# One pool moved ahead of another and the compressions moved to later projections, in a hybrid NSA and HGRN2 decoder layer

## The chip, the cores and the metric

The kernel runs on one core of one Trainium2 chip. The metric is the device time of one execution in microseconds (us), taken on that core. The kernel before was run three times for it: a median of 1119.54 us, from 1118.82 to 1120.39. One further execution was recorded by the hardware profiler; all rows below come from it.

The engines are named as in the profile: PE (TensorE: matmuls; PEld is its loading of weights), DVE (VectorE), ACT (ScalarE), POOL (GpSimd) and SP (SyncE, which here only issues DMAs). SPq, ACTq and POOLq are the DMA issues of these engines.

## What is computed

One decoder layer on x of 512 tokens by 2048. Cut to what matters here:

```python
h = rmsnorm(x, norm_in)
proj = h @ w_in                      # 2048 x 7728: q, six K/V pieces, gates, z, and HGRN2's q, f, i, z
kc = compress_blocks(k_cmp, pe_k, w1_k, w2_k)   # 31 blocks of 32 tokens, (blk + pe) -> gelu(@ w1) @ w2
vc = compress_blocks(v_cmp, pe_v, w1_v, w2_v)
o_a = attention over compressed, selected and windowed tokens   # 16 heads of 64, 4 K/V groups
o_h = hgrn2_mixer(q_h, f_h, i_h, lb)                            # 8 heads of 128, chunks of 64
mixed = concat(head_rmsnorm(o_a) * silu(z_a), head_rmsnorm(o_h) * silu(z_h))
out = rmsnorm(x + mixed @ w_out, final_norm)
```

Everything is float32, and the result has to agree with float32 arithmetic.

## The kernel before

**Products in three parts.** A float32 matmul of the projections is done as three faster ones: each operand is split into a high part and a low remainder (hi and lo), and the product is hi·hi + hi·lo + lo·hi. The transposed, normalised input is held as `hh0` to `hh3` (high) and `hl0` to `hl3` (low): eight tiles of 8192 bytes per partition (the function `b8`, pool "big"). A piece of the projection's weights is loaded by SP into a tile `w` of 4096 bytes (`load_raw`, L163; pool "w", `b4`), split by ACT (high part, L304) and DVE (low part, L305) into two more tiles `w`, and used by PE. There are ten tiles in that pool, so a load waits for a tile to come free.

**Three forms of projection.** In `proj_fm` (L545) `w` is the stationary operand and 512 columns (2048 bytes) of an `hh` or `hl` tile stream past it: L559, L560 and L561, `pj<-hh,w` in the rows, where the moving operand stands first and the weights second. One projection of 128 columns is 16 such triples in two halves of weights, 48 matmuls. In `proj_tm` (L566; L584 to L586) it is the other way: 128 columns of `hh` or `hl` are the weights, and `w` streams. `seven` (L456 to L458, L466 to L468) computes two of the projections from seven products instead of eight; it too streams `w`, past weights that are pieces of `hh` and `hl` or sums of such pieces in tiles `s`. Late in the kernel `hh2`, `hl2`, `hh3` and `hl3` hold the mixed result instead, for the output projection.

**Where the tiles lie.** Pools of tiles are laid out in the order of their creation: "const", then "big" (64 KiB per partition), then "small" (2,624 bytes of little tiles, `sm`), then the pools that come later, "w" among them. `hh0` therefore begins 65,536 + 2,624 = 68,160 bytes ahead of the first tile `w`. That is 133 × 512 + 64: since tiles `w`, `hh` and `hl` and the columns in them step by multiples of 512 bytes here, a piece of `w` that is used as weights lies 64 bytes past a multiple of 512 from the `hh` or `hl` columns that stream at that time, and the other way round in `proj_tm` (448 past one). The tiles `s` lie multiples of 512 from the tiles `w`.

**Order of the work.** `run` (L114) weaves generators: each yields an estimated cost after a piece of work, and the one that is furthest behind in cost divided by its weight goes next. The order in which instructions are written is the order of each engine's queue. From 271.5 us on the stage between the first projections and the attention runs (L1163 to L1177):

- `blocks` (L605) gathers the raw K (or V) to be compressed from DRAM into four tiles by eight DMAs (L611 to L614), for K on ACT's queue, for V on POOL's, clears a few columns (L619, POOL) and adds the position term, 16 operations on DVE (L625).
- `compress` (L629) loads the first weight matrix in four pieces (L632, SP) and the second (L637, SP), does 64 matmul records of 128x128 (L641), a gelu on ACT and DVE (L647 to L652), and the second product: L657 for K, which gives `kc_hi` and `kc_lo` (L659, L660), L670 for V (from two copies by ACT, L664).
- `make_q` and `make_kd` each do one projection by `proj_fm` and then `split_dma` (L683): one operation of DVE, one of ACT, one of DVE (L686 to L688) and DMAs on SP (L691). `make_kd(0, 1)` moreover copies `kc_hi` and `kc_lo` with POOL into the tiles `kw` (L711, L712), which the first scores read (L779).
- `rows_back` (L1076) reads values back from DRAM; here for `v_tok`, four DMAs on POOL's queue.

In the kernel before, the K compression is woven into kd00 and q0 (`make_kd(0, 0)` and `make_q(0)`, 22 : 10), the V compression into kd01, q1, kd10 and q2 (44 : 44). Then the attention of 16 heads is woven with the other projections as its filling (160 : 102): q3, kd11, q4 to q7 and `hgrn_qf(0)`, ten projections of 48 matmuls.

Of the kernel before, what the change touches and what calls it, by code (L numbers as in the profile page):

```python
# [48 lines left out]
def hymba_layer(ctx: ExitStack, tc: tile.TileContext, x, norm_in, w_in, pe_k, w1_k, w2_k,  # L49
                pe_v, w1_v, w2_v, lower_bounds, nsa_norm, hgrn_norm, w_out, final_norm, out):  # L50
    nc = tc.nc
# [3 lines left out]
    w_out2 = w_out.rearrange("l d c -> (l d) c")  # L55

    const = ctx.enter_context(tc.tile_pool(name="const", bufs=1))
    big = ctx.enter_context(tc.tile_pool(name="big", bufs=1))
    small = ctx.enter_context(tc.tile_pool(name="small", bufs=2))
    psum = ctx.enter_context(tc.tile_pool(name="psum", bufs=1, space=bass.MemoryType.PSUM))  # L60

    cnt = [0, 0, 0]
# [1 line left out]
    def nm(s):  # L64
        cnt[0] += 1
        return f"{s}_{cnt[0]}"
# [8 lines left out]
    def sl(dt=FP32):  # L75
        return space["slab"].tile([P, 512], dt, name=nm("s"), tag="s", bufs=NSLAB)
# [35 lines left out]
    def run(*gens):  # L112

        st = [[g, t, 0.0] for g, t in gens]  # L114
        while st:
            e = min(st, key=lambda e: e[2] / e[1])
            try:
                c = next(e[0])
                e[2] = max([o[2] / o[1] for o in st if o is not e]) * e[1] + 1e-6 if c is None else e[2] + c
            except StopIteration:  # L120
                st.remove(e)

    def chain(*gens):
        for g in gens:
            yield from g
# [479 lines left out]
    def blocks(acc, pcol, eng):  # L605

        kv = []
        for j in range(2):
            f = acc[j]
            e, o = sl(), sl()  # L610
            eng.dma_start(out=e[0:64, :], in_=f[0:64, :])  # L611
            eng.dma_start(out=e[64:128, 0:511], in_=f[0:64, 1:512])
            eng.dma_start(out=o[0:64, :], in_=f[64:128, :])
            eng.dma_start(out=o[64:128, 0:511], in_=f[64:128, 1:512])  # L614
            kv += [e, o]
        blk = [sl() for _ in range(4)]
        for uq in range(4):
            b4_ = blk[uq].rearrange("p (u g n) -> p u g n", u=4, g=4)
            nc.gpsimd.memset(b4_[:, :, :, 31:32], 0.0)  # L619
            pe = col[:, pcol + uq * 4:pcol + uq * 4 + 4].unsqueeze(2).broadcast_to([P, 4, 31])  # L620
            for g in range(4):
                src = kv[g].rearrange("p (n u two) -> p u n two", u=8, two=2)
                n0 = uq // 2
                sv = src[:, (uq % 2) * 4:(uq % 2) * 4 + 4, n0:n0 + 31, 0]
                nc.vector.tensor_tensor(b4_[:, :, g, 0:31], sv, pe, ALU.add)  # L625
        return blk
# [70 lines left out]
    def make_kd(g2, b):  # L697


        acc = []  # L700
        yield from proj_fm(acc, (C_KS, C_KW)[b] + g2 * P, P)
        if b == 0:
            t = [sl(F32R) for _ in range(4)]
            v = t
        else:
            t = [space["att"].tile([P, 672], F32R, name=nm("kw"), tag="kw", bufs=KWB) for _ in range(4)]
            v = [a[:, 160:672] for a in t]
            for i in range(4):
                g = 2 * g2 + i // 2
                src = (kc_hi, kc_lo)[i % 2]  # L710
                nc.gpsimd.tensor_copy(t[i][:, 0:P], kd[g][0][i % 2][:, 0:P].bitcast(FP32))  # L711
                nc.gpsimd.tensor_copy(t[i][:, P:160], src[:, g * 32:(g + 1) * 32].bitcast(FP32))  # L712
        split_dma(acc[0], 1.0, [(v[0], 0, 0, 0), (v[0], 1, 0, 0), (v[1], 0, 1, 0), (v[1], 1, 1, 0),
                                (v[2], 0, 0, 1), (v[2], 1, 0, 1), (v[3], 0, 1, 1), (v[3], 1, 1, 1)])
        kd[2 * g2][b], kd[2 * g2 + 1][b] = t[0:2], t[2:4]

    def make_q(p):
        acc = []
        yield from proj_fm(acc, C_Q + p * P, P)
        qe, qo = sl(F32R), sl(F32R)  # L720
        split_dma(acc[0], -DH ** -0.5, [(qe, 0, 0, 0), (qe, 1, 1, 0), (qo, 0, 0, 1), (qo, 1, 1, 1)])
        q2[2 * p], q2[2 * p + 1] = qe, qo
# [127 lines left out]
    def attention():  # L850
        units = [(h, i, b) for h in range(HEADS) for i in range(NT) for b in ((0, 1) if i else (None,))]
        es, ys_, behind = {}, {}, []

        def step(gen):
            return next(gen, None)

        for u in range(len(units) + AHEAD):
            if u < len(units):
                h, i, b = units[u]
                while q2[h] is None or kd[h // 4][1] is None:  # L860
                    yield None
                if h not in es:
                    es[h] = head_setup(h)
                ys_[u] = scores(es[h], i, b)
                yield (0.4, 0.24, 0.33, 0.44)[i]
            v = u - AHEAD
            if v >= 0:
                h, i, b = units[v]
                flip(es[h], i, b, ys_.pop(v))
                yield 0.11 * max(i + 1, 2)  # L870
                if behind:
                    c = next(behind[0], None)
                    if c is None:
                        behind.pop(0)
                    else:
                        yield c
                if b == 1 and i == 3:
                    weigh(es[h])
                    yield 2.5
                    behind.append(head_out(es.pop(h)))  # L880
                    if h % 4 == 3:
                        behind.append(attn_cmp(h // 4))
        for g in behind:
            yield from g
# [188 lines left out]
    def rows_back(scr_, alloc, eng=nc.sync):  # L1073
        tiles = [alloc() for _ in range(NT)]
        for t in range(NT):
            eng.dma_start(out=tiles[t], in_=scr_[t])  # L1076
        return tiles
# [74 lines left out]
    KC, VC, vf = [], [], []  # L1152
# [15 lines left out]
    kblk = blocks(kf, 32, nc.scalar)  # L1168
    masks()
    vc_bd += [sl() for _ in range(2)]  # L1170
    for v in vc_bd:
        nc.gpsimd.memset(v, 0.0)
    run((chain(make_kd(0, 0), make_q(0)), 22), (compress(kblk, w1_k, w2_k, True), 10))
    v_tok += rows_back(vt_scr, sl, nc.gpsimd)
    vblk = blocks(vf, 48, nc.gpsimd)
    run((chain(make_kd(0, 1), make_q(1), make_kd(1, 0), make_q(2)), 44), (compress(vblk, w1_v, w2_v, False), 44))
    fill = [make_q(3), make_kd(1, 1)] + [make_q(p) for p in range(4, 8)]  # L1177
    with tc.tile_pool(name="pt", bufs=2) as space["pt"]:
        run((attention(), 160), (chain(*fill, hgrn_qf(0)), 102))
    att.close()  # L1180
    space["late"] = ctx.enter_context(tc.tile_pool(name="late", bufs=NLATE))
    hv[0] = rows_back(v_scr[0], late)
# [1 line left out]
    fill = chain(hgrn_qf(1), hgrn_qf(2), hgrn_qf(3), z_proj(C_ZH, sz[2]))  # L1184
# [77 lines left out]
    for c in range(3):  # L1262
# [3 lines left out]
        p = proj_tm([], w_out2, mT, c * 512, 512, out_done(c))  # L1266
# [35 lines left out]
```

## Time and profile before

| | us |
|---|---|
| median of three runs (range) | 1119.54 (1118.82 to 1120.39) |
| the profiled execution | 1119.59 |
| span of its trace, first to last instruction | 1117.9 |
| PE busy in the span | 1087.6 (97%) |
| DVE busy | 659.5 (59%) |
| ACT busy | 419.9 (38%) |
| POOL busy | 95.3 (9%) |
| mean granted clock of TensorE | 0.993 of 2.4 GHz |

The span is divided below into stages by time: input and first projections to 97 us, `seven` to 271.5, the stage with the two compressions to 369, attention with its filling to 615, the HGRN2 heads with theirs to 925, then gates, z and output projections. A matmul's length in the rows is the time that it is in the array, some 0.39 us for 512 columns; since matmuls follow each other in a pipeline, the distance from one start to the next is what one costs.

### The profile page before, as it was taken

Reading aid. Unit: us, or ns where it says so; the run is one execution under the profiler, and the core shown is the slowest. Engines: PE = TensorE matmul, PEld = TensorE weight load, DVE = VectorE, ACT = ScalarE, POOL = GpSimd, SP = SyncE. Lnnn points to the kernel's source line nnn. Section 1 sums busy time; section 2 is a strip of 40 time slices with the busy share of each in tenths; the row PEclk is TensorE's granted clock in tenths of the full one; section 3 lists DMA queues with packets and bytes.
Section 4 is the critical chain, followed back from the end, with each engine's and each line's share of the span. In section 5 each row is a group of like instructions: output and inputs, shape, how many; then the busy total and the mean of one; then the engine's idle time right before and its main releaser. Section 6 shows DMA issues by size and latency. Waiting matters only on the chain.

```text
span 1117.9 us, 15221 instructions
## 1 busy us (share of the span) xinstructions
PE 1087.6 (97%) x5610; PEld 885.0 (79%) x5610; DVE 659.5 (59%) x1549; ACT 419.9 (38%) x835; POOL 95.3 (9%) x170
## 2 busy tenths in 40 slices
PE   7999999999889999999999999999999999999996
PEld 6799888888768777777677788888888788888886
DVE  4766757663434567675656466666667789424333
ACT  6534443341113555564544222222232443323212
POOL 1000000102310102020200000000000000102010
PEclk9999999999989999999999999999999999999998
DMA  9435346545565422222112223222121723235223
GB/s 316 143 113 170 104 144 214 166 141 171 159 180 152 132 57 57 57 76 57 39 39 71 80 76 97 76 74 76 57 76 57 245 76 119 97 116 176 96 85 123
DMA packets 100010, 127.45 MB, mean 114 GB/s; under 512 B 6672, under 2 KB 62368, under 8 KB 99936
## 3 DMA queue, kind: packets, MB, share of 16 engines
q1 hardware_dynamic: 94368, 113.90, 33.2%
q0 software_dynamic: 2624, 8.39, 2.2%
q10 hardware_dynamic: 2944, 4.19, 1.1%
q8 instruction: 44, 0.72, 0.3%
q14 instruction: 30, 0.25, 0.1%
HBM read 106.01 MB, written 12.06 MB: 106 GB/s over the span
## 4 chain that ended last, share of the span: by engine, by line
PE 88%; DVE 4%; issue 3%; DMA 2%; POOL 1%; ACT 1%; SPq 1%; ACTq 0%; POOLq 0%
PE pj L559 8%; PE pj L560 8%; PE pj L561 8%; PE pj L585 7%; PE pj L584 7%; PE pj L586 7%; PE ot L826 4%; PE pj L807 3%; PE lp L975 3%; PE pj L457 2%; PE pj L456 2%; PE pj L458 2%; DMA w<-in_w_in_dram 2%; PE lp L793 2%; PE lp L794 2%
## 5 line engine op out<-in xcount | busy, mean ns | idle before, releaser
L305 DVE TENSOR_TENSOR w<-w,w 128x1024 fp32r<-128x1024 f32 (+3 forms) x169 | 204.5, 1215 | 169.5 <-ACT w L304 76.0
L304 ACT CAST w<-w 128x1024 fp32r<-128x1024 f32 (+3 forms) x169 | 172.9, 1036 | 273.1 <-DMA w<-in_w_in_dram 137.8
L559 PE MATMUL pj<-hh,w 128*128 128x512 f32 x448 | 184.6, 412 | 4.9 <-ACT w L304 4.9
L560 PE MATMUL pj<-hl,w 128*128 128x512 f32 x448 | 180.6, 403 | 0.0
L561 PE MATMUL pj<-hh,w 128*128 128x512 f32 x448 | 179.6, 401 | 0.0
L584 PE MATMUL pj<-w,hh 128*128 128x512 f32 (+2 forms) x352 | 127.2, 361 | 0.0
L585 PE MATMUL pj<-w,hl 128*128 128x512 f32 (+2 forms) x352 | 126.2, 358 | 0.0
L586 PE MATMUL pj<-w,hh 128*128 128x512 f32 (+2 forms) x352 | 125.4, 356 | 0.0
L559 PEld LDWEIGHTS pj<-hh,w 128*128 128x128 f32 x448 | 84.8, 189 | 25.1 <-ACT w L304 5.4
L561 PEld LDWEIGHTS pj<-hh,w 128*128 128x128 f32 x448 | 84.7, 189 | 20.4 <-issue 1.3
L560 PEld LDWEIGHTS pj<-hl,w 128*128 128x128 f32 x448 | 84.8, 189 | 17.3 <-issue 1.0
L762 DVE CUSTOM_DVE_ANT_0 s<-s,lp 128x128 f32<-128x128 f32 (+3 forms) x128 | 60.3, 482 | 40.9 <-PE lp L794 30.1
L767 ACT ACTIVATE s<-s,mn 128x128 f32<-128x128 f32 (+3 forms) x128 | 71.6, 560 | 33.6 <-DVE mn L762 25.8
L586 PEld LDWEIGHTS pj<-w,hh 128*128 128x128 f32 x352 | 66.2, 188 | 8.9
L584 PEld LDWEIGHTS pj<-w,hh 128*128 128x128 f32 x352 | 66.2, 188 | 8.7
L585 PEld LDWEIGHTS pj<-w,hl 128*128 128x128 f32 x352 | 66.2, 188 | 8.0
L807 PE MATMUL pj<-ident,s 128*128 128x128 f32 x320 | 54.6, 276 | 1.0 <-ACT s L767 1.0
L826 PE MATMUL ot<-pt,s 128*64 128x512 f32 (+3 forms) x256 | 49.9, 441 | 0.8 <-DVE pt L818 0.8
L807 PEld LDWEIGHTS pj<-ident,s 128*128 128x128 f32 x320 | 39.6, 140 | 11.6 <-ACT s L767 5.3
L826 PEld LDWEIGHTS ot<-pt,s 128*64 128x64 f32 x256 | 24.4, 136 | 21.3 <-issue 9.4
L816 ACT COPY pt<-pj 128x256 f32<-128x256 f32 (+2 forms) x56 | 25.6, 457 | 41.3 <-PE pj L807 40.7
L584 PE MATMUL pj<-w,s 128*128 128x512 f32 x96 | 37.7, 393 | 0.0
(346 smaller groups left out, 1914.8 us busy)
## 6 DMA issues: line engine op xcount, KB each, us to landing
w<-in_w_in_dram SPq DMA_DIRECT2D x121, 512.0 KB, 3.5
w<-in_w_out_dram SPq DMA_DIRECT2D x32, 512.0 KB, 3.6
s<-s SPq DMA_DIRECT2D x48, 128.0 KB, 2.3
w<-in_x_dram SPq DMA_DIRECT2D x16, 256.0 KB, 6.5
d<-e POOLq DMA_DIRECT2D x12, 256.0 KB, 2.9
l<-in_x_dram SPq DMA_DIRECT2D x12, 256.0 KB, 5.1
out_dram<-l SPq DMA_DIRECT2D x12, 256.0 KB, 3.1
w<-in_w_in_dram SPq DMA_DIRECT2D x5, 456.0 KB, 3.3
```

The source lines that it names most:

```text
L304: nc.scalar.copy(hi, raw)
L305: nc.vector.tensor_tensor(lo, raw, hi.bitcast(FP32), ALU.subtract)
L559: nc.tensor.matmul(acc[j], wh, hh, start=kk == 0, stop=False)
L560: nc.tensor.matmul(acc[j], wh, hl, start=False, stop=False)
L561: nc.tensor.matmul(acc[j], wl, hh, start=False, stop=kk == NK - 1)
L584: nc.tensor.matmul(o, ah, hi[:, k, :], start=kk == 0, stop=False)
L585: nc.tensor.matmul(o, al, hi[:, k, :], start=False, stop=False)
L586: nc.tensor.matmul(o, ah, lo[:, k, :], start=False, stop=kk == NK - 1)
L762: nc.vector.tensor_tensor_reduce(out=y, in0=e["bias"][:, 384 - i * P:512], in1=lp, scale=1.0, scalar=3e38, op0=ALU.add, op1=ALU.min, accum ...
L767: nc.scalar.activation(y, y, AF.Exp, bias=mn, scale=-1.0, accum_out=e["ls"][:, 2 * i + b:2 * i + b + 1])
L807: nc.tensor.transpose(tps[:, j * P:(j + 1) * P], y[:, j * P:(j + 1) * P], ident)
L826: nc.tensor.matmul(e["ot"][b * 64:(b + 1) * 64, j * P:512], v_tok[j][:, b * 256 + g * DH:b * 256 + (g + 1) * DH], e["pt"][:, b, j * 512:38 ...
```

## The change

The pool "small" is created ahead of "big". `hh0` moves back by 2,624 bytes, the tiles `w` stay where they are, and `hh0` lies 65,536 = 16 × 4096 bytes ahead of the first `w`. And the stage of the compressions is woven otherwise: kd00 and q0 alone, q1 with the K compression, kd01 and q2 with the V compression; kd10 becomes the first piece of the attention's filling (weight 113 instead of 102); the V blocks are gathered ahead of `v_tok` on POOL's queue.

```diff
     const = ctx.enter_context(tc.tile_pool(name="const", bufs=1))
+    small = ctx.enter_context(tc.tile_pool(name="small", bufs=2))
     big = ctx.enter_context(tc.tile_pool(name="big", bufs=1))
-    small = ctx.enter_context(tc.tile_pool(name="small", bufs=2))
     psum = ctx.enter_context(tc.tile_pool(name="psum", bufs=1, space=bass.MemoryType.PSUM))
@@ -1170,13 +1170,14 @@
-    run((chain(make_kd(0, 0), make_q(0)), 22), (compress(kblk, w1_k, w2_k, True), 10))
+    run((chain(make_kd(0, 0), make_q(0)), 22))
+    run((make_q(1), 11), (compress(kblk, w1_k, w2_k, True), 10))
+    vblk = blocks(vf, 48, nc.gpsimd)
     v_tok += rows_back(vt_scr, sl, nc.gpsimd)
-    vblk = blocks(vf, 48, nc.gpsimd)
-    run((chain(make_kd(0, 1), make_q(1), make_kd(1, 0), make_q(2)), 44), (compress(vblk, w1_v, w2_v, False), 44))
-    fill = [make_q(3), make_kd(1, 1)] + [make_q(p) for p in range(4, 8)]
+    run((chain(make_kd(0, 1), make_q(2)), 22), (compress(vblk, w1_v, w2_v, False), 22))
+    fill = [make_kd(1, 0), make_q(3), make_kd(1, 1)] + [make_q(p) for p in range(4, 8)]
     with tc.tile_pool(name="pt", bufs=2) as space["pt"]:
-        run((attention(), 160), (chain(*fill, hgrn_qf(0)), 102))
+        run((attention(), 160), (chain(*fill, hgrn_qf(0)), 113))
```

Lines from L1174 on are one further down in the changed kernel. Three places show how instructions move.

**PE, the first matmuls of the K compression** (L641; `pj_422` is kd00's accumulator, `pj_448` is q1's). Before:

```order
L561 MATMUL pj_422_2442<-hh3_21_144,w_433_2501 128x512
L559 MATMUL pj_422_2442<-hh3_21_144,w_432_2500 128x512
L560 MATMUL pj_422_2442<-hl3_22_145,w_432_2500 128x512
L641 MATMUL lp_428_2466<-s_414_2376,w_426_2461 128x128
L641 MATMUL lp_429_2467<-s_414_2376,w_426_2461 128x128
```

After:

```order
L561 MATMUL pj_448_2594<-hh0_15_138,w_451_2598 128x512
L559 MATMUL pj_448_2594<-hh0_15_138,w_450_2597 128x512
L560 MATMUL pj_448_2594<-hl0_16_139,w_450_2597 128x512
L561 MATMUL pj_448_2594<-hh0_15_138,w_451_2598 128x512
L641 MATMUL lp_454_2618<-s_414_2376,w_452_2613 128x128
```

Before, 41 matmuls of kd00 stand ahead of the first L641; in the changed kernel all 96 of kd00 and q0 and 12 of q1 do.

**POOL, from the copies of `kc` to the V blocks.** Before:

```order
L712 CAST kw_487_2830<-kc_hi_184 128x32
L712 CAST kw_489_2832<-kc_hi_184 128x32
L712 CAST kw_488_2831<-kc_lo_185 128x32
L712 CAST kw_490_2833<-kc_lo_185 128x32
L1076 DMA s_457_2652<-d_53_180 128x512
L1076 DMA s_458_2653<-d_54_181 128x512
L1076 DMA s_459_2654<-d_55_182 128x512
L1076 DMA s_460_2655<-d_56_183 128x512
L611 DMA s_461_2660<-d_146_674 64x512
L612 DMA s_461_2660<-d_146_674 64x511
```

After:

```order
L712 CAST kw_499_2903<-kc_hi_184 128x32
L712 CAST kw_501_2905<-kc_hi_184 128x32
L712 CAST kw_500_2904<-kc_lo_185 128x32
L712 CAST kw_502_2906<-kc_lo_185 128x32
L611 DMA s_469_2725<-d_146_674 64x512
L612 DMA s_469_2725<-d_146_674 64x511
L613 DMA s_470_2726<-d_146_674 64x512
L614 DMA s_470_2726<-d_146_674 64x511
L611 DMA s_471_2731<-d_147_675 64x512
L612 DMA s_471_2731<-d_147_675 64x511
```

The V blocks' DMAs stand directly behind the copies of `kc_hi` and `kc_lo` in both, but now ahead of `v_tok`.

**PE, the first matmuls of the V compression** (`pj_494` is q1's accumulator before, `pj_481` is kd01's and `pj_506` q2's in the changed kernel). Before:

```order
L561 MATMUL pj_494_2856<-hh1_17_140,w_497_2860 128x512
L559 MATMUL pj_494_2856<-hh1_17_140,w_496_2859 128x512
L560 MATMUL pj_494_2856<-hl1_18_141,w_496_2859 128x512
L641 MATMUL lp_475_2719<-s_465_2672,w_473_2715 128x128
L641 MATMUL lp_476_2720<-s_465_2672,w_473_2715 128x128
```

After:

```order
L561 MATMUL pj_481_2769<-hh3_21_144,w_494_2847 128x512
L559 MATMUL pj_506_2929<-hh0_15_138,w_508_2932 128x512
L560 MATMUL pj_506_2929<-hl0_16_139,w_508_2932 128x512
L561 MATMUL pj_506_2929<-hh0_15_138,w_509_2933 128x512
L559 MATMUL pj_506_2929<-hh0_15_138,w_508_2932 128x512
L641 MATMUL lp_487_2792<-s_473_2737,w_485_2788 128x128
```

Between the K compression's last product (L657) and this point there were 80 matmuls of 512 columns, and there are 52 now (48 of kd01, 4 of q2); behind its 64 come the remaining 44 of q2, with the second product (L670) after the 16th of them, and then the first scores (L779).

## Rows read from the trace of the kernel before

**Rows 1.** The page's first part: engines, busy us, share of the span, instructions.
```profile
PE 1087.6 (97%) x5610; PEld 885.0 (79%) x5610; DVE 659.5 (59%) x1549; ACT 419.9 (38%) x835; POOL 95.3 (9%) x170
```
**Rows 2.** Stretches: length, busy (count) of PE, PEld, DVE, ACT, POOL; PEclk, DMA, GB/s.
```profile
271.50:369.00 97.50, 87.91 (x437) 73.17 (x436) 37.37 (x70) 18.57 (x30) 27.36 (x67) 0.95 0.63 175
369.00:615.00 246.00, 243.13 (x1339) 182.43 (x1338) 164.29 (x505) 136.03 (x363) 29.83 (x49) 1.00 0.23 62
```
**Rows 3.** The same view, behind the two idle times of PE.
```profile
285.85:289.00 3.15, 3.15 (x15) 3.15 (x16) 0.65 (x3) 0.00 (x0) 1.54 (x3) 0.51 0.00 0
...
318.50:323.10 4.60, 4.56 (x10) 3.19 (x11) 1.21 (x1) 0.35 (x1) 0.00 (x0) 0.51 0.98 251
```
**Rows 4.** Timeline of PE: start, length, what, idle before.
```profile
285.85 7.06 PE L641 MATMUL lp<-s,w 128*128 128x128 f32 x48 [4.62 <-POOL s L288]
...
318.50 0.80 PE L559 MATMUL pj<-hh,w 128*128 128x512 f32 x1 [4.93 <-ACT w L304]
```
**Rows 5.** Timeline of ACT and DVE ahead of the first idle time.
```profile
276.45 1.51 ACTq L614 DMA_DIRECT2D s<-d  x1
...
280.19 6.31 DVE L625 TENSOR_TENSOR s<-s,col 128x124 f32<-128x124 f32 x15 [4.01 <-DMA s<-d]
```
**Rows 6.** The chain of waits, 271 to 345 us: start, length, what.
```profile
303.75 0.45 SPq L632
304.30 13.09 DMA w<-in_w_in_dram
...
331.31 7.14 PE lp L641 x64
```
**Rows 7.** Timeline of PE in `seven`.
```profile
205.76 0.39 PE L456 MATMUL pj<-w,hh 128*128 128x512 f32 x1
...
211.26 0.39 PE L456 MATMUL pj<-w,s 128*128 128x512 f32 x1
211.49 0.39 PE L457 MATMUL pj<-w,s 128*128 128x512 f32 x1
211.71 0.39 PE L458 MATMUL pj<-w,s 128*128 128x512 f32 x1
...
213.98 0.39 PE L456 MATMUL pj<-w,hh 128*128 128x512 f32 x1
```
**Rows 8.** Timeline of PE in kd00.
```profile
273.13 0.39 PE L560 MATMUL pj<-hl,w 128*128 128x512 f32 x1
...
280.83 0.40 PE L560 MATMUL pj<-hl,w 128*128 128x512 f32 x1
```
**Rows 9.** The page's fifth part: `proj_fm`'s second matmul, busy and mean ns.
```profile
L560 PE MATMUL pj<-hl,w 128*128 128x512 f32 x448 | 180.6, 403 | 0.0
```
**Rows 10.** PE matmuls that read `hl`, by stretch: length, busy (count), PEclk, DMA, GB/s.
```profile
97.00:271.50 174.50, 74.47 (x198) 1.00 0.46 151
...
615.00:925.00 310.00, 136.81 (x341) 1.00 0.29 91
925.00:1080.00 155.00, 48.87 (x124) 1.00 0.33 112
```
**Rows 11.** Timeline of PE, POOL and DVE: from `kc` to the V blocks.
```profile
304.58 0.61 PE L657 MATMUL tp<-s,s 128*128 128x128 f32 x4
...
306.19 2.17 POOL L1076 DMA_DIRECT2D s<-d  x4
308.35 0.54 POOL L611 DMA_DIRECT2D s<-d  x1
324.98 4.51 DVE L625 TENSOR_TENSOR s<-s,col 128x124 f32<-128x124 f32 x16
```
**Rows 12.** DMA issues, 271 to 325 us: count, KB each, median us to landing.
```profile
s<-d POOLq DMA_DIRECT2D x4, 128.0 KB, 7.2
```
**Rows 13.** Timeline of ACT and SP behind the V compression's L641.
```profile
341.50 1.14 ACT L664 COPY s<-s 128x512 f32<-128x512 f32 x2 [1.05 <-DVE s L652]
...
343.19 2.39 SPq L691 DMA_DIRECT2D kw<-s  x4
```

## The prediction

> **What bounds the kernel now.** I began with the engines: PE is busy for 97% of the span, DVE for 59% [rows 1], so time is won only where PE idles or where a matmul gets cheaper. The table by stretches says where PE idles: in the stage of the two compressions it is busy 87.91 of 97.50 us, at a mean clock of 0.95, in the attention stage 243.13 of 246 at 1.00 [rows 2]. PE's timeline shows two waits in that stage, 4.62 us ahead of the first L641 and 4.93 us at 318.50 [rows 4]. Behind each, the clock granted is 0.51, the lower of the two levels (1.2 of 2.4 GHz) [rows 3]. The third thing to read is the distance from one matmul's start to the next's. All matmuls in [rows 7, 8] run at the full clock, are 512 columns wide and never wait, yet they differ:
> - `w` streaming past weights in `s` (a multiple of 512 bytes away): 12 from 211.26 to 213.98, 2.72 us, **226.7 ns** each.
> - the same lines, `w` streaming past weights in `hh` or `hl` (448 past a multiple of 512): 24 from 205.76 to 211.26, 5.50 us, **229.2 ns**.
> - `hh` and `hl` streaming past weights in `w` (64 past a multiple): 33 from 273.13 to 280.83, 7.70 us, **233.3 ns**.
>
> So the cost goes with where the weights of the next matmul, loaded meanwhile, lie against the operand that is streaming. After the change both kinds of pair lie multiples of 512 apart.
>
> **Part A, the small pool ahead of the big one.** The instructions and their bytes stay the same; only addresses change. In `proj_fm` there are 448 triples [rows 9], 1,344 matmuls at 233.3; if they cost 226.7 to 226.8, that is 6.5 ns each, 8.7 us. Of the second kind, where `hh` or `hl` are weights, there is one matmul on `hl` in each triple: 160 of 512 columns in `seven` (198 less the 38 of a narrower projection), 341 less 218 of `proj_fm` = 123, and 124 [rows 10], together 407 triples or 1,221 matmuls at 2.4 ns: 2.9 us. In the last 38 us, and for the 96 of the second projection, I allow 0.5 (bounds 0 and 1.5). Not all reaches the end: of `proj_fm`'s matmuls 528 (eleven projections of 48) fill gaps in the attention, where exponentials and transposes follow each other; PE idles only 2.9 of 246 us there [rows 2], so most counts, and I take off a third, 1.1 us. A = 8.7 + 2.9 + 0.5 − 1.1 = **11.0 us**. Bounds: nothing, if the distance in bytes is not the cause, and 13.5, if all of it comes through.
>
> The trace thus says that loading weights can slow the matmul that runs beside it. The Trainium skill says otherwise: "TensorE: Matmul & The Clock Gate", section "Step-by-step: what each phase is for", has it that PE has two independent read ports and that loading the next tile's weights takes no read bandwidth from the running matmul. By that rule A is nothing, and the time 1109.4. [Rows 7] speak against it, with 2.5 ns between two kinds of weights past the same moving tiles.
>
> **Part B, the compressions beside later projections.** What it removes, each from [rows 3, 4, 6]:
> - the wait ahead of L641, 4.62. The row names POOL, but the blocks' last DMA is issued at 276.45 and the adds go on from 280.19 for 6.31 us, when they have the data [rows 5]. They are done at 286.5; in the changed kernel 96 + 12 matmuls stand ahead, and from 271.5 that is 271.5 + 108 × 0.227 = 296.0. The adds are covered with some 9 us to spare.
> - the slow clock behind it: 48 records took 7.06; 64 take 7.14 later [rows 6], so 48 should take 5.36. 1.7.
> - the wait at 318.50, 4.93: a half of kd01's weights, issued at 304.30 behind three loads of V's compression weights (the last 303.75), needs 13.09 us [rows 6]. Now the K compression's 64 records and q1 stand between q0 and kd01, so SP reaches that load while PE has some 18 us of work in hand (48 × 0.227 + 64 × 0.1116). It costs nothing.
> - the slow clock behind that: ten matmuls in 4.60 us [rows 3] that cost 2.33 at 233.3. 2.3.
>
> Together 13.55. What it adds:
> - kd10 (48 matmuls, 10.9 us, and its split) moves into the attention, and the weights 113 to 160 keep both ending together. PE's work is the same; it costs nothing while PE bounds that stage. If the attention's own chains did, it would cost up to its share of PE's 2.9 idle us.
> - **The V blocks are wanted sooner.** POOL's queue holds their DMAs behind L712, which waits for `kc`. From L657 to the end of L712 it takes 1.6 us (304.58 to 306.19), eight issues take 4.3 at 0.54, then landing, then four of the adds (16 take 4.51, so 1.1) [rows 11]: 7.0 and the landing. `v_tok` no longer stands in between, which saves its 2.17. Landing took 7.2 us before [rows 12], amid other loads; as a floor I set 3, an estimate, under half of that. The first L641 of V may thus run 10.0 to 14.2 us behind L657, plus 1.2 if DVE's split of the next weights goes first. PE has 48 + 4 matmuls in between, 11.8 us (before, 80). The wait is 0 to 3.6; I take **2.5**, near the row, since loads of q2's weights and of V's compression weights still run beside it.
> - The second products, each behind a gelu: ACT ends its copies (L664) 4.2 us after L641's end at 338.45 [rows 6, 13], with 16 matmuls (3.6) in between; 0.6 there, and 0.2 for K's. **0.8**.
> - The first scores need `kw`, whose DMAs are issued by 345.58, 7.1 behind the end of L641 [rows 13]; with my floor of 3 for landing that is 10.1. PE has 44 matmuls in between, 10.0 us, and the records of L670 on top. Nothing, but with little to spare; with a landing of 7.2 it would be some 2.5.
>
> B = 13.55 − 2.5 − 0.8 = **10.2 us** (bounds 4.3, with both waits at their worst and the slow clock once, and 13.5).
>
> **Sum.** The profiled execution took 1119.59 us, 1.7 more than its span and 0.05 over the median, so no correction is needed: 1119.6 − 11.0 − 10.2 = 1098.4; I say **1098**.
>
> **The rivals.**
> 1. *Addresses matter less than I read.* Two cases. The distance is no cause at all and only B comes: 1119.6 − 10.2 = 1109.4; against it stand [rows 7], the same lines and the same moving tiles with two prices. Or only the second kind gains: in [rows 8] another operand streams, and its 233.3 may belong to that operand rather than to the distance; then A is 3 and the time 1106. No row shows `hh` streaming at a multiple of 512, which is why this keeps a chance: 0.08 for the first, 0.06 for the second. The rule of the Trainium skill above is the first case.
> 2. *A new wait takes the place of the old one.* The V blocks land 7.2 us behind their last issue, with DVE's split ahead: 3.6 us, and behind it the clock drops for another 2.3, as it did behind both waits before [rows 3, 4]. B falls to 13.55 − 5.9 − 0.8 = 6.9 and the time is 1101.7, or 1104 with a late `kw` too. For it: a landing as slow as this was measured; against it: two of the loads that ran beside it come earlier now. 0.12, at 1103.
> 3. *Slower: weights and stream collide at multiples of 4096.* The new distance is not only a multiple of 512 but of 4096, and if a load of weights that far off held up the stream more than one 64 bytes past does, all 2,565 matmuls of A would pay. From 10.2 / 2565 = 4 ns over their present price on, B is eaten up; at the 6.6 ns between the cheapest and the dearest pair above, paid once more, it is 17 us: 1119.6 − 10.2 + 17 = 1126. Against it: the matmul at 211.49 streams a `w` while weights are loaded that lie an exact multiple of 4096 from it, and the next starts 0.22 us later [rows 7]. 0.04.
> 4. *It doesn't do what it says:* the attention swallows kd10 badly and loses what part B won there (PE idle beyond 2.9 us in that stage), A still comes: 1119.6 − 11.0 = 1108.6. Against it: the stage's PE is busy to 243.13 of 246 [rows 2], and a filling that is longer by one piece gives it no new wait. 0.04.
>
> **How the numbers follow.** The forecast has 0.66, with a range of its own from 1093 (no new wait, all of A) to 1102. The whole range runs to 1110, to take in rivals 1 and 2. About 0.2%, 2.2 us, is what a measurement of this kernel tells from no change; the forecast and rivals 1, 2 and 4 lie far below that line. Faster 0.92, same 0.03, slower 0.05.
>
> **What would show it.** In the profile after: L559 to L561 start 227 ns apart instead of 233, and L584 to L586 and `seven` beside `hh` weights 227 instead of 229 (part A); no idle time ahead of K's first L641, none at kd01, and a clock of 1.00 through that stage (part B); a wait of 1 to 4 us ahead of V's first L641, released by DVE's adds; none ahead of L779. It is wrong if those distances stay at 233, if the wait ahead of V's L641 is over 4 us with a slow clock behind it, or if PE idles in the attention markedly more than 2.9 us.

## The result, and the profile after

The changed kernel takes **1102.06 us** (median of four runs, 1100.78 to 1103.47) against 1119.26 of the kernel before beside it: a ratio of 0.9845, 95% interval 0.9828 to 0.9862. Run once more in a later set it came to 0.9858 (0.9838 to 0.9878). The forecast was 1098, in a range of 1093 to 1110: the sign and the size hold, 17 us instead of 21. The time lies 0.06 us above the forecast's own range (1093 to 1102), though, and nearer to rival 2 (1101.7 to 1104) than to 1098. How the 17 us come about is another matter.

The page's first part of the changed kernel, profiled in an execution of 1100.78 us:

```profile
span 1099.1 us, 15254 instructions
...
PE 1073.5 (98%) x5610; PEld 883.3 (80%) x5610; DVE 658.8 (60%) x1549; ACT 419.6 (38%) x835; POOL 95.5 (9%) x170
```

PE does the same 5,610 matmul records in 14 us less busy time than in [rows 1]. Next the distances from start to start, in PE's timeline of the changed kernel:

```profile
205.08 0.39 PE L456 MATMUL pj<-w,hh 128*128 128x512 f32 x1
...
210.52 0.39 PE L456 MATMUL pj<-w,s 128*128 128x512 f32 x1
...
213.24 0.39 PE L456 MATMUL pj<-w,hh 128*128 128x512 f32 x1
...
271.04 0.39 PE L559 MATMUL pj<-hh,w 128*128 128x512 f32 x1
...
278.52 0.39 PE L559 MATMUL pj<-hh,w 128*128 128x512 f32 x1
```

24 matmuls beside `hh` and `hl` weights from 205.08 to 210.52 are 226.7 ns each (229.2 in [rows 7]); 12 beside `s` weights, to 213.24, still 226.7; 33 of kd00 in 7.48 us, 226.7 as well (233.3 in [rows 8]). Three prices have become one.

The stages, in the table by stretches: length, then busy time of PE, PEld, DVE, ACT and POOL, granted clock, DMA share, GB/s. The first is kd00's start to the first scores, the second from there to the first HGRN2 matmul.

```profile
270.40:349.00 78.60, 74.47 (x389) 63.63 (x388) 32.91 (x66) 16.73 (x28) 30.02 (x67) 0.96 0.70 204
349.00:622.70 273.70, 271.19 (x1486) 208.27 (x1484) 174.87 (x522) 141.16 (x369) 27.92 (x50) 1.00 0.26 70
```

The first answers to the first of [rows 2]. The second in the kernel before, to the same point of the program:

```profile
369.00:638.30 269.30, 266.31 (x1438) 200.63 (x1436) 173.61 (x520) 140.69 (x368) 30.16 (x51) 1.00 0.24 65
```

The compression stage is 18.9 us shorter, of which 11.2 is kd10 (48 matmuls at 233.3), moved out: 7.7 us won. The mean clock there, 0.96, is hardly better. The attention took kd10 in and is only 4.4 us longer. Why the clock did not recover is in the timelines of PE and DVE and in the chain of waits of the changed kernel:

```profile
323.91 0.50 PE L559 MATMUL pj<-hh,w 128*128 128x512 f32 x1 [2.15 <-ACT w L304]
...
325.17 0.50 PE L561 MATMUL pj<-hh,w 128*128 128x512 f32 x1 [0.52 <-DVE w L305]
...
327.38 9.86 PE L641 MATMUL lp<-s,w 128*128 128x128 f32 x64 [1.46 <-issue]
```

```profile
323.88 1.22 DVE L305 TENSOR_TENSOR w<-w,w 128x1024 fp32r<-128x1024 f32 x1 [5.45 <-ACT w L304]
325.03 3.85 DVE L625 TENSOR_TENSOR s<-s,col 128x124 f32<-128x124 f32 x14
```

```profile
314.40 8.31 DMA w<-in_w_in_dram
322.81 1.05 ACT w L304
323.88 1.24 DVE w L305
```

Both old waits are gone [rows 4], and two new ones have come, closer together, the first in two pieces. The first half of q2's weights, issued at 314.40 behind q1's split on SP, lands 8.31 us later; PE idles 2.15 us for its high part and 0.52 for its low part. Four matmuls after the first of these it idles again, 1.46 us. The row names no releaser; it is the adds of the V blocks, 14 of 16 of which DVE runs behind the split of those weights: in all five traces with this wait (the changed kernel twice, `e2_weave_only`, `e6_kd10_ahead`, `e7_vtok_late`) L641 starts 2.34 to 2.36 us behind the first of the 14. The three waits are 4.1 us together. Behind them the clock falls and V's 64 records of L641 take 9.86 us instead of 7.14 [rows 6]:

```profile
320.00:325.00 5.00, 2.49 (x10) 1.42 (x8) 1.11 (x1) 1.04 (x1) 0.00 (x0) 1.00 1.08 347
...
325.00:331.00 6.00, 4.38 (x19) 3.95 (x20) 5.01 (x16) 1.04 (x1) 0.00 (x0) 0.56 0.42 122
331.00:337.40 6.40, 6.40 (x51) 6.36 (x51) 1.22 (x1) 1.40 (x3) 0.00 (x0) 0.88 0.29 82
```

### The profile page after: what moved, and what is told of

It is laid out like the page before. It is cut to its first block, busy times and chain, and to the rows that moved or that the text cites. A ratio compares the mean times of both kernels' runs of the same rounds, so it can differ in the third digit from the quotient of the medians.

```text
span 1099.1 us, 15254 instructions
## 1 busy us (share of the span) xinstructions
PE 1073.5 (98%) x5610; PEld 883.3 (80%) x5610; DVE 658.8 (60%) x1549; ACT 419.6 (38%) x835; POOL 95.5 (9%) x170
## 3 DMA queue, kind: packets, MB, share of 16 engines
q0 software_dynamic: 2624, 8.39, 2.1%
## 4 chain that ended last, share of the span: by engine, by line
PE 90%; DVE 5%; DMA 2%; issue 2%; ACT 1%; SPq 0%; ACTq 0%; POOL 0%; DVEq 0%; POOLq 0%
PE pj L559 8%; PE pj L560 8%; PE pj L561 8%; PE pj L584 7%; PE pj L586 7%; PE pj L585 7%; PE ot L826 4%; PE pj L807 3%; PE lp L975 2%; PE pj L458 2%; PE pj L457 2%; PE pj L456 2%; PE lp L793 2%; PE lp L641 2%; PE lp L794 1%
## 5 line engine op out<-in xcount | busy, mean ns | idle before, releaser
L304 ACT CAST w<-w 128x1024 fp32r<-128x1024 f32 (+3 forms) x169 | 173.0, 1036 | 276.3 <-DMA w<-in_w_in_dram 148.4
L559 PE MATMUL pj<-hh,w 128*128 128x512 f32 x448 | 183.5, 410 | 2.8 <-ACT w L304 2.2
L561 PE MATMUL pj<-hh,w 128*128 128x512 f32 x448 | 176.7, 394 | 0.5 <-DVE w L305 0.5
L586 PE MATMUL pj<-w,hh 128*128 128x512 f32 (+2 forms) x352 | 125.6, 357 | 0.0
L559 PEld LDWEIGHTS pj<-hh,w 128*128 128x128 f32 x448 | 84.3, 188 | 21.1 <-issue 2.9
L561 PEld LDWEIGHTS pj<-hh,w 128*128 128x128 f32 x448 | 84.2, 188 | 19.0 <-issue 1.2
L586 PEld LDWEIGHTS pj<-w,hh 128*128 128x128 f32 x352 | 66.5, 189 | 8.5
L826 PE MATMUL ot<-pt,s 128*64 128x512 f32 (+3 forms) x256 | 47.3, 440 | 0.0
```

The costliest lines, as they stand in the source:

```text
L304: nc.scalar.copy(hi, raw)
L559: nc.tensor.matmul(acc[j], wh, hh, start=kk == 0, stop=False)
L561: nc.tensor.matmul(acc[j], wl, hh, start=False, stop=kk == NK - 1)
L586: nc.tensor.matmul(o, ah, lo[:, k, :], start=False, stop=kk == NK - 1)
L826: nc.tensor.matmul(e["ot"][b * 64:(b + 1) * 64, j * P:512], v_tok[j][:, b * 256 + g * DH:b * 256 + (g + 1) * DH], e["pt"][:, b, j * 512:38 ...
```

## The experiments

Line numbers of a kernel that adds lines are shifted: by two in `e4_pad192`, `e5_pad64` and `e11_pad128` (L561 there is L559 here, L588 is L586), by four behind `blocks` in `e9_q2_inside` and `e10_gather_early` (L645 there is L641 here).

### The two parts alone

`e1_pool_only` is the first hunk of the change without the second, `e2_weave_only` the second without the first.

> Only the small pool is moved ahead of the big one; the old order of work stays. Theory 1 (the price of a matmul goes with the distance, modulo 512 bytes, between the weights loaded and the operand streaming): the pairs of L559 to L561 go from 233 to 227 ns, seven's from 229 to 227, both old waits of the compression stage (some 5 us each) stay, and the time is 1119.3 less 1.1 (seven), 1.9 (compression stage), 3.4 (everything behind the attention) and the attention's share. That share is 2.3 us, and the time 1110.6, if the other 4 us that the attention won in the changed kernel came from the new order; it is 6.7 us, and the time 1106, if they came from the addresses. Theory 2 (addresses don't matter, the order of work did it all): 1119.

> Only the new order of work; the small pool stays behind the big one. Theory 1: pairs stay at 233 and 229 ns. The compression stage without kd10 is some 6 us shorter than before (two waits of 5 us and their slow clock gone, two new waits of 2.5 and 1.9 us and a slow clock behind them come instead), and the time is 1113; 1109 if the attention's extra 4 us come from the order. Theory 2: 1102, as the whole change.

Measured: the pool alone **0.9937** (0.9917 to 0.9956), the order alone **0.9914** (0.9892 to 0.9936). On 1119.3 that is −7.1 and −9.6, together −16.7 of the 17.3: the parts add up, and each is needed. Theory 2 falls with the pairs of the pool alone, 227 ns at the old order. Of theory 1's two cases the one in which the attention's extra 4 us come from the order fits both times (1112.2 beside 1110.6, 1109.7 beside 1109).

But neither part is what was forecast. The tables by stretches, of the pool alone and of the order alone:

```profile
270.10:367.30 97.20, 86.88 (x437) 73.71 (x436) 37.52 (x70) 18.58 (x30) 27.20 (x66) 0.93 0.64 176
367.30:635.40 268.10, 265.06 (x1439) 200.46 (x1438) 173.08 (x520) 140.66 (x368) 30.81 (x52) 1.00 0.24 66
```

```profile
271.20:353.30 82.10, 76.62 (x389) 63.87 (x388) 33.01 (x66) 16.80 (x28) 29.71 (x67) 0.94 0.67 195
353.30:628.70 275.40, 273.10 (x1486) 208.46 (x1484) 174.90 (x522) 141.22 (x369) 27.83 (x50) 1.00 0.26 70
```

With cheaper matmuls alone the compression stage keeps its length, 97.20 against 97.50: 288 matmuls save 1.9 us, and PE then waits for the same transfers. Its two waits have grown by 0.73 us together, and behind them PE works 9.0 instead of 7.6 us at the lower clock (granted 0.5), which costs another 0.7:

```profile
284.79 7.41 PE L641 MATMUL lp<-s,w 128*128 128x128 f32 x48 [5.23 <-POOL s L288]
...
317.46 0.80 PE L559 MATMUL pj<-hh,w 128*128 128x512 f32 x1 [5.05 <-ACT w L304]
```

The attention gains 1.2 us, where 480 matmuls at 6.5 ns would make 3.1. Behind it, from the first HGRN2 matmul to the last of `proj_fm`, the two traces matched instruction by instruction give 1.0 us: from one projection matmul to the next 2.16 us are won in 517 steps, and 0.94 is lost in the 45 steps from a projection to a head's own matmul, where PE now stands a little longer. The gain of the 517 steps, 3.4 us at 6.6 ns each, recurs in the changed kernel, `e3_mult512` and `e4_pad192` (2.1 to 2.3 us); the loss varies there from 0.1 to 1.9. Part of why the 517 steps give no more shows in the changed kernel's timeline, behind a run of narrow matmuls:

```profile
622.71 1.57 PE L975 MATMUL lp<-s,s 128*128 128x192 f32 x8 [0.20 <-POOL s L990]
...
624.35 0.40 PE L561 MATMUL pj<-hh,w 128*128 128x512 f32 x1
...
625.28 0.39 PE L559 MATMUL pj<-hh,w 128*128 128x512 f32 x1
...
626.41 0.40 PE L561 MATMUL pj<-hh,w 128*128 128x512 f32 x1
```

The first four starts from 624.35 on are 232 ns apart, the next five 226. In the stage as a whole the second to fourth matmul of a run cost 232 to 233 with either layout, and those from the twelfth on 226.7 after and 233.4 before. A run that is cut often gains little.

With the new order alone the compression stage is 15.4 us shorter, 4.2 beside kd10, not 10 (the new waits are 4.45 us for q2's weights and 0.99 for the V blocks in that trace); and the attention with kd10 is 6.1 us longer instead of 11.2. So 5 us of part B come from a place where none was expected.

### What moving kd10 is worth

```diff
-    fill = [make_kd(1, 0), make_q(3), make_kd(1, 1)] + [make_q(p) for p in range(4, 8)]
+    run((make_kd(1, 0), 11))
+    fill = [make_q(3), make_kd(1, 1)] + [make_q(p) for p in range(4, 8)]
...
-        run((attention(), 160), (chain(*fill, hgrn_qf(0)), 113))
+        run((attention(), 160), (chain(*fill, hgrn_qf(0)), 102))
```

> The whole change, but kd10 stays ahead of the attention, by itself, and the filling's weight is 102 as before. Theory F (the attention hides waits that the profile's idle time doesn't show, and kd10 fills them): the compression stage grows by kd10's 10.9 us, the attention shrinks by only some 6, and the time is about 5 us over the whole change, ratio to before 0.989. Rival P (PE is full in the attention, so kd10 costs the same on either side): the time of the whole change within 1 us, ratio 0.9845.

Measured: **0.9884** (0.9866 to 0.9901), as theory F has it. The stages of this kernel:

```profile
271.30:362.10 90.80, 85.89 (x438) 72.93 (x437) 36.37 (x70) 19.40 (x31) 29.28 (x67) 0.96 0.70 200
362.10:630.40 268.30, 265.20 (x1439) 200.71 (x1437) 170.92 (x519) 138.96 (x366) 30.78 (x51) 1.00 0.24 64
```

Ahead of the attention the stage is 12.2 us longer with kd10 (90.80 against 78.60): 10.9 are kd10's 48 matmuls, the rest is for the most part that the new waits (2.71 us instead of 2.15 ahead of q2) and the slow clock behind them were longer in this trace. Inside the attention kd10 costs 5.4 (273.70 against 268.30). The two traces thus put the gain at 5.5 us, the ratios of the times (0.9884 against 0.9845 and 0.9858) at 3 to 4.4. PE idles 3.1 us without it and 2.5 with it; the time that kd10 fills there is nowhere shown as idle, since a matmul's row lasts 0.39 us (its time in the array) while the next may start 0.23 us after it, so a wait of a tenth of a microsecond lies under the row before it. Taken from start to start, the steps of this stage that are longer than the shortest tenth between the same two shapes are so by 57 us together without kd10 and by 54 with it: there is room that no row shows, though this does not tell waits from what else makes a step long. Nor does this kernel tell kd10's presence from the other weave that came with it: its filling differs in weight (102, not 113) and in its first piece as well.

### The new waits

Three kernels built on the changed one. `e7_vtok_late` issues the four loads of `v_tok` behind the V compression; `e8_vblk_early` does that and gathers the V blocks ahead of the K compression; `e10_gather_early` leaves `v_tok` where the change puts it, issues only the V blocks' DMAs ahead of the K compression and keeps the adds behind it:

```diff
+    vkv = blocks(vf, nc.gpsimd)
     run((make_q(1), 11), (compress(kblk, w1_k, w2_k, True), 10))
-    vblk = blocks(vf, 48, nc.gpsimd)
+    vblk = add_pe(vkv, 48)
     v_tok += rows_back(vt_scr, sl, nc.gpsimd)
```

For it `blocks` is split in two: what is left of it issues the DMAs, and `add_pe` does the adds.

> The whole change, but the four loads of v_tok are issued behind the V compression. Theory C (the two new waits, 2.5 us for q2's weights and 1.9 us for the V blocks, come from too many transfers in flight): q2's first weights land some 2 us sooner, the wait for them falls under 0.5 us, the clock stays at 1.00 through V's L641 (64 records in 7.1 us, not 9.9), and the time falls by 4 to 6 us, ratio 0.980. Rival S (they come from SP, which issues that load only behind q1's split): the wait stays at 2 us or more and the time within 1 us of the whole change.

Measured: 0.983 (0.9813 to 0.9847), not to be told from the whole change, and the waits stand:

```profile
324.18 0.50 PE L559 MATMUL pj<-hh,w 128*128 128x512 f32 x1 [2.44 <-ACT w L304]
...
327.65 9.96 PE L641 MATMUL lp<-s,w 128*128 128x128 f32 x64 [1.47 <-issue]
```

Theory C is wrong as far as `v_tok`'s transfers go. That the wait stays is what rival S says; no run issued that load earlier on SP, so its cause is not shown.

> The whole change, but the V blocks are gathered ahead of the K compression (on POOL's queue ahead of the copies of kc), and v_tok is issued behind the V compression. Theory C: both new waits go and with them the slow clock, 2.3 + 1.6 + 2.7 = 6.6 us, and the time is about 1095.5, ratio 0.979. Rival S: the wait for q2's weights stays, the one for the blocks goes: 1 to 3 us better than the whole change, ratio 0.982 to 0.984.

Measured: 0.9824 (0.9807 to 0.9842), the time that rival S gave, but not for its reason: both waits and the slow clock are gone, as theory C had it, and the stage is 5.2 us shorter. Another wait came: DVE runs V's adds ahead of the K compression's gelu, and K's second product waits 2.13 us (timelines of DVE and PE):

```profile
306.38 3.90 DVE L625 TENSOR_TENSOR s<-s,col 128x124 f32<-128x124 f32 x14
310.20 0.42 DVE L648 TENSOR_TENSOR s<-s 128x256 f32<-128x256 f32 x1
...
312.37 0.71 PE L657 MATMUL tp<-s,s 128*128 128x128 f32 x4 [2.13 <-DVE s L652]
```

And the attention gave 3.8 us back (277.45 from the first scores to the first HGRN2 matmul). With `v_tok` late, thirteen triples of filling instead of eight stand ahead of the first head's transposes, which start 9.67 us behind the scores instead of 6.27. That this is the cause is not shown: `e7_vtok_late` starts them at 9.44 and takes 2.0 us more than the changed kernel, `e6_kd10_ahead` at 8.54 and loses nothing against `e1_pool_only` (268.3 and 268.1, 5.64 there).

> The whole change, but the V blocks' DMAs are issued ahead of the K compression; their adds stay behind it, and v_tok stays where the change puts it. Theory C: no wait ahead of V's L641 nor for q2's weights, clock 1.00, and no delay of the K compression's gelu: the compression stage takes 71 to 73 us instead of 78.7 and the attention 273 to 275 as in the changed kernel; ratio 0.978. Rival A (what the stage wins is given back at the start of the attention, whose first head waits for something of its own): the attention takes 277 or more, ratio 0.982 or more.

Measured: **0.9756** (0.9734 to 0.9779), 1094.7 us, about 1% under the change itself (0.9845 and 0.9858), and the best kernel of this study. Its stages:

```profile
270.20:342.10 71.90, 71.65 (x389) 61.50 (x388) 31.29 (x65) 16.56 (x28) 30.53 (x67) 1.00 0.80 230
342.10:616.10 274.00, 271.37 (x1487) 207.54 (x1485) 175.91 (x523) 141.28 (x369) 28.24 (x50) 1.00 0.26 68
```

PE's rows fill the compression stage (71.65 of 71.90) at a clock of 1.00, and the attention is as in the changed kernel. The two new waits and the slow clock behind them were worth 6.7 us of span (78.60 − 71.90); the ratios say 10 to 11 us, the spans of the profiled executions 5.3 to 6.5, and the traces place no more than the 6.7. With V's blocks early, V's 64 records stand beside kd01 instead of behind it:

```profile
314.27 3.73 PE L645 MATMUL lp<-s,w 128*128 128x128 f32 x32
...
319.68 3.73 PE L645 MATMUL lp<-s,w 128*128 128x128 f32 x32
```

So q2's weights are wanted some 9 us later as well (331.1 us instead of 321.6): one edit removes both waits, and this kernel cannot say what each alone would have left. The `run` line that weaves V's compression is the same in both kernels, word for word. That the order of writing is the order of each engine's queue, as the section on the kernel before has it, is thus not the whole: moving the DMAs moved PE's matmuls.

### More filling still

`e9_q2_inside` goes on from there: the K compression beside kd01, the V compression beside q1, and q2 too moves into the attention (weight 124).

```diff
-    run((make_q(1), 11), (compress(kblk, w1_k, w2_k, True), 10))
+    run((make_kd(0, 1), 11), (compress(kblk, w1_k, w2_k, True), 10))
...
-    run((chain(make_kd(0, 1), make_q(2)), 22), (compress(vblk, w1_v, w2_v, False), 22))
+    run((make_q(1), 11), (compress(vblk, w1_v, w2_v, False), 11))
...
-    fill = [make_kd(1, 0), make_q(3), make_kd(1, 1)] + [make_q(p) for p in range(4, 8)]
+    fill = [make_q(2), make_kd(1, 0), make_q(3), make_kd(1, 1)] + [make_q(p) for p in range(4, 8)]
```

> Built on the changed kernel: the V blocks' DMAs are issued ahead of the K compression, the adds behind it; the K compression stands beside kd01, the V compression beside q1, and q2 becomes the first piece of the attention's filling (weight 124). Theory F (the attention hides waits that filling fills): q2 costs some 5.5 us there instead of 10.9, and the new waits and the slow clock (6.6 us) are gone: ratio to before about 0.974, 1090 us on the scale of 1119.3. Rival P (the attention is full by now): q2 costs 10.9 there, ratio 0.978 to 0.979.

Measured: 0.9836 (0.9813 to 0.9859): 0.8% over `e10_gather_early`, against both theories.

```profile
270.00:331.70 61.70, 60.91 (x342) 52.32 (x340) 26.25 (x57) 11.85 (x20) 28.77 (x67) 1.00 0.80 234
331.70:623.20 291.50, 285.94 (x1535) 219.78 (x1534) 181.80 (x532) 145.09 (x377) 27.93 (x49) 1.00 0.27 71
```

The stage ahead is 10.2 us shorter, as it should be, but the attention 17.5 longer, with twice the idle time. The attention's own last matmul (L914 of the kernel before) starts 276.3 us behind the first score instead of 253.3, so it is the heads' own work that was drawn out. One piece of filling costs 5.4 there, a second, put first, more than its own length. Whether the room is used up or the weights interleave badly was not tried apart.

### What distance counts

Four layouts at the old order of work. `e3_mult512` puts the tag `la` (128 bytes) into a pool of its own ahead of "big" and 64 bytes behind "small"; the others put 192 (shown here), 64 and 128 bytes behind "small":

```diff
+    gap = ctx.enter_context(tc.tile_pool(name="gap", bufs=1))
+    gap.tile([P, 48], FP32, name="gap", tag="gap", bufs=1)
```

> Old order of work; one tag of the small pool (128 bytes) goes ahead of the big pool and 64 bytes are put behind it, so that hh0 lies 68,096 bytes ahead of the first w: 133 times 512, but not a multiple of 4096. Theory 1 (modulo 512 is what counts): the same time as with the pool moved, within 1 us, and pairs at 227 ns. Theory 3 (the multiple of 4096 is what counts): pairs stay near 233 and the time at 1119.

> Old order of work; 192 bytes are put behind the small pool, so that the distance is 133.5 times 512: weights lie 256 past a multiple of 512 from the operand streaming, a distance that no row of before shows. Theory 1a (only an exact multiple is cheap): pairs of L559 to L561 at 231 to 235 ns, time 1118 to 1121. Theory 1b (the price grows with the distance from a multiple, 64 away is only the beginning): pairs above 235 ns, time over 1123. Theory 1c (what counts is a multiple of 256): 227 ns and the time of the pool moved.

> Old order of work; 64 bytes are put behind the small pool, so that the weights lie 128 bytes past a multiple of 512 from the operand streaming (0 and 256 past one gave pairs at 227 ns, 64 and 448 gave 233 and 229). Theory M128 (multiples of 128 are cheap): pairs of L559 to L561 at 227 ns, a time some 5 us under before, as with 256. Theory M256: pairs at 230 to 234 ns and the time of before within 2 us.

> Old order of work; 128 bytes are put behind the small pool: the weights w lie 192 past a multiple of 256 from the operand streaming, and the hh weights 64 past one, the mirror of before. Theory M256 (the price is set by the distance modulo 256: 0 gives 227 ns, 64 gives 233.3, 128 gives 232.4, 192 gives 229): pairs of L559 to L561 at 229, pairs of L584 to L586 and seven beside hh weights at 233; 1344 at -4.3 and 1221 at +4 ns nearly cancel, and the time is that of before within 2 us. Rival (each kind of operand has a price of its own off the multiples, whatever the distance): 233 and 229 as before.

Means from start to start: 33 matmuls at kd00's beginning, and the 479 steps of `seven` beside `hh` and `hl` weights, all 512 columns wide at the full clock.

| run | `w` as weights: past a multiple of 256 | ns | `hh` as weights: past one | ns | ratio to before |
|---|---|---|---|---|---|
| `e1_pool_only` | 0 (0 past 4096) | 226.7 | 0 | 226.7 | 0.9937 (0.9917 to 0.9956) |
| `e3_mult512` | 0 (0 past 512) | 226.7 | 0 | 226.7 | 0.9955 (0.994 to 0.997) |
| `e4_pad192` | 0 (256 past 512) | 226.7 | 0 | 226.7 | 0.9957 (0.9939 to 0.9974) |
| before | 64 | 233.3 | 192 | 228.9 | 1 |
| `e5_pad64` | 128 | 232.4 | 128 | 232.5 | 1.0031 (1.0021 to 1.0041) |
| `e11_pad128` | 192 | 229.3 | 64 | 233.2 | 1.0015 (1.0003 to 1.0027) |

Timelines of PE that two of these prices come from, in `e4_pad192` (27 starts in 6.12 us) and in `e11_pad128` (33 in kd00, 7.56 us; 18 in `seven` beside `hh`, 4.20 us):

```profile
271.79 0.39 PE L561 MATMUL pj<-hh,w 128*128 128x512 f32 x1
...
277.91 0.39 PE L561 MATMUL pj<-hh,w 128*128 128x512 f32 x1
```

```profile
206.57 0.40 PE L458 MATMUL pj<-w,hh 128*128 128x512 f32 x1
...
210.77 0.40 PE L458 MATMUL ot<-w,hh 128*128 128x512 f32 x1
...
273.96 0.39 PE L561 MATMUL pj<-hh,w 128*128 128x512 f32 x1
...
281.52 0.39 PE L561 MATMUL pj<-hh,w 128*128 128x512 f32 x1
```

Neither 4096 (`e3_mult512`) nor 512 (`e4_pad192`) is the unit: a multiple of 256 suffices; 128 doesn't. Off a multiple the price goes with the signed distance: 64 past gives 233 whichever operand streams, 192 past gives 229. `e11_pad128`, the mirror of before, swaps the two prices between the two kinds of matmul, which excludes a price that belongs to an operand. Theory M256 holds for the prices in every row. Its time for `e5_pad64`, that of before within 2 us, missed: 3.5 us more (2.4 to 4.6), since the second kind of matmul rose from 228.9 to 232.5 ns, which on its 1,221 matmuls is 4.4 us, while the first kind gained 1.2. So the times follow the prices. `e3_mult512` and `e4_pad192`, expected within 1 us of `e1_pool_only`, gain 2 us less at the same prices; the intervals overlap, and no run here shows whether it is more than noise.

### The change once more

> The changed kernel once more, as it is, to set its ratio beside those of the other runs: 0.983 to 0.986 of before, if the ratios of different calls can be compared.

Measured: 0.9858 (0.9838 to 0.9878), within what was expected, with the new waits again: 3.53 and 0.28 us for q2's weights and 1.00 for the V blocks.

## Why the prediction was right, and where it was not

**Part A, the price of a pair: right.** 233.3 and 229 became 226.7, as the 12 matmuls beside `s` had shown. Rival 1 is out in both its cases, by the pool moved alone and by the mirror. Its first case was the rule of the Trainium skill, "TensorE: Matmul & The Clock Gate", section "Step-by-step: what each phase is for", that loading the next weights takes no read bandwidth from the matmul that runs. The traces disagree: up to 6.6 ns in 227, in long runs, and in all six layouts of the table the price goes with the distance between the two operands.

**Part A, its size: too large.** I took 6.5 ns off nearly every matmul and a third off in the attention, 11.0 us; alone it measures 7.1 (4.9 to 9.3), and 5.3 between the two profiled executions. The failed step is "most counts": in the compression stage 1.6 of 1.9 us went into longer waits for the same transfers and the slow clock behind them; in the attention 1.2 of 3.1 came through; among the HGRN2 heads 1.0 of 3.7 (562 steps at 6.6 ns). The discount belonged to every stage where projections fill gaps, not to one.

**Part B, what goes: right.** Both waits of [rows 4] and the slow clock behind them are gone. The clock of 1.00 through the stage, which was to show it, did not come.

**Part B, what comes: half the price.** "The V blocks are wanted sooner" was right as a place: I took 2.5 us for that wait, with the clock kept, and 0.8 ahead of the second products, where no row of PE shows a wait (L657, L670). What came was 1.5 us for the blocks and 2.7 in two pieces a few matmuls earlier, for q2's weights, which I had counted only as work for DVE ahead of the adds and not as something PE itself would wait for. Behind both the clock fell to 0.56. That is rival 2's pattern, a new wait with the slow clock behind it, with another transfer at its head. Together 6.7 us by `e10_gather_early`, against my 3.3. A wait of over 4 us ahead of V's L641 with a slow clock behind it was to be a sign of being wrong: the wait there is 1.46, but with those for q2's weights it is 4.1, and the slow clock came.

**Part B, kd10: wrong, in the kernel's favour.** "PE's work is the same; it costs nothing" compared equal with equal; in fact kd10's 48 matmuls are 10.9 us ahead of the attention and cost 5.4 inside. I read 2.9 us of idle time in 246 [rows 2] as a full engine. In `e2_weave_only` the compression stage gave 4.2 us where 10.2 stood, and the attention 5.1 where nothing stood; the two errors nearly cancel, and B came to 9.6 (7.2 to 12.1). That this sum was right is luck; the 4 us by which the total is off are A's.

**Rival 3**, a collision at multiples of 4096, did not come: exact multiples of 4096, of 512 and of 256 cost the same. **Rival 4** had the attention lose by kd10; it won.

## What to carry to other kernels

Measure a matmul from start to start and group those distances by where the operands lie: where weights and streaming operand stand a multiple of 256 bytes apart, 512-column float32 matmuls ran 1 to 3% faster here; 192 bytes of padding bought the same price, and 4.8 us of the kernel's time beside 7.1 by the pool. Do not read PE's busy share as proof that a stage is full: in a stage that weaves chains with filling, waits shorter than a matmul's row lie under the rows, and moving a piece in and out of it tells what it costs there. And when a wait is removed, ask of every transfer that the following work needs when it can now be issued, not only of the one that was late.

## What was not expected of the hardware

The price off a multiple of 256 has a sign (64 past 233, 128 past 232, 192 past 229). For 256 columns the order is reversed: 12 starts take 1.44 us in the changed kernel, where the weights lie at a multiple of 256, and 1.36 in `e11_pad128`, where they lie 64 past one (113 against 120 ns). Timelines of the two:

```profile
65.80 0.28 PE L586 MATMUL pj<-w,hh 128*128 128x256 f32 x1
...
67.24 0.28 PE L586 MATMUL pj<-w,hh 128*128 128x256 f32 x1
```

```profile
65.79 0.28 PE L588 MATMUL pj<-w,hh 128*128 128x256 f32 x1
...
67.15 0.28 PE L588 MATMUL pj<-w,hh 128*128 128x256 f32 x1
```

So the layout that is best for wide matmuls costs these narrow ones 6% against that of `e11_pad128`, and 2% against before (191 steps: 120.0 against 113.5 and 117.8 ns; 118.7 in `e5_pad64`). And the first three or four 512-column matmuls behind a run of narrow ones cost 232 to 233 ns among the HGRN2 heads, with the old layout and with the new; no run here shows why.
